# The attention prologue of a two-layer block: the kv, k_pe and query down-projections in an order written by hand

## The chip, the core and the metric

The kernel runs on one core of a Trainium2 chip. The metric is device time in microseconds (us) of one execution. TensorE (PE) does the matrix products, PEld is its weight load, VectorE (DVE) and ScalarE (ACT) do the elementwise work and read the products out of PSUM, GpSimd (POOL) does a few copies, and SyncE (SP) issues the transfers.

## The reference, cut to what matters

Two layers run over x (512 tokens of 1024 features) and a context (256 tokens). Layer 0 mixes tokens by Fourier and Hyena branches; layer 1 is latent attention, whose prologue is changed. `hx` and `hc` are the normalized and modulated rows of x and of the context.

```python
a_x = hx @ w_in                      # 256 query + 128 kv + 32 pe columns
q_x = _mla_queries(a_x[..., :256], *q_args, rope)
k_x, v_x = _mla_keys_values(a_x[..., 256:], *kv_args, rope)
a_c = hc @ w_in[:, 256:]             # the context needs kv and pe only
k_c, v_c = _mla_keys_values(a_c, *kv_args, None)
...
q   = _rms_norm(a_q, q_a_norm) @ w_uq        # latent norm over 256
ckv = _rms_norm(a_kv[..., :128], kv_a_norm)  # latent norm over 128
kv  = ckv @ w_ukv                            # keys (nope part) and values
```

Then 16 heads attend to 768 keys, the result is projected and added to x, and a gated convolutional FFN follows.

## The kernel before, in words

Features lie on partitions and tokens on the free dimension: the eight row tiles `hh[0..7]` and `hl[0..7]` (the high and the low part of h) hold 128 features each, of 512 tokens, two zero columns, 256 context tokens and two zero columns (772 in all). The context is columns 514 to 769, and its products take columns 512 to 771 (260). Every product is made of three matmuls by `mm3` (lines 121 to 125): high weight by high data (L123), high weight by low data (L124), low weight by high data (L125). A weight is loaded by `wraw`, and `wsplit` makes its two parts: ScalarE casts the high part (`hi`, L98), VectorE subtracts it for the low part (`lo`, L103). Raw, high and low weights have three buffers each.

The order of instructions on each engine is set by a scheduler that plans with its own costs, and the program's order is only one of its inputs; instructions of one engine then run strictly in the order that it wrote. PSUM has three `mm` tiles of 1024 columns and two `ms` tiles of 512.

The FFN of layer 0 ends with `norm_hook` (L283): its hook makes the first norm of layer 1 for the 512 tokens of x, and what it returns as `rest` makes the norm of the context: eight squares and sums (L233, L234), the copy of the sums, their transposes and the root (L244, L248, L250, `rsqrt` from L127), the spread of the root over the partitions (L256), and eight rows of scaled, high and low parts (L266, L267, L271).

`attention` (L959) then does, in the program's order:
- loads and splits of w_kv and w_pe (L985 on), tables for rotary embedding;
- `down(0, T)` (L1006): for each of the eight rows the kv product and the pe product, into the PSUM tiles pkv and ppe;
- `rest()`, the norm of the context;
- `latent(0, T)` (L1013): `small_norm` (L934) of kv (square L940, sum L941, copy L943, transposes L947, root L949, spread L953, copy L955), the scaling L1016, and its high and low parts kvh and kvl;
- the query products, two weights of eight rows each, into pqa;
- `down(512, 260)` and `latent(C0, C)` for the context;
- `small_norm` of the query latent, its scaling (L1044) and parts qah and qal;
- the pe part: square L1048, kp L1050, sums L1053, rotation L1058, high and low parts Kh and Kl, and POOL's copies of them (L1083);
- `values`: six token blocks by w_v (two of 512 columns each, copied out at L1028), with the load of w_uk between blocks 0 to 3 and blocks 4 and 5.

Behind it the PSUM pool is replaced, and `qk(p)` (L1091) makes queries (out `s`) and keys (out `k`) of head pair p, with two pairs made ahead of the loop over pairs.

Of the kernel before, what the change touches and what calls it, by code (L numbers as in the profile page):

```python
# [9 lines left out]
F32 = mybir.dt.float32  # L10
# [3 lines left out]
AF = mybir.ActivationFunctionType  # L14
ALU = mybir.AluOpType
# [3 lines left out]
P = 128  # L19
D = 1024  # L20
KD = 8
T = 512
C = 256
C0 = 514
# [3 lines left out]
EPS = 1e-6  # L28
# [22 lines left out]
class Builder:  # L51
# [169 lines left out]
    def norm(self, i, k, x, hh, hl, c0, n, tp):  # L221
# [31 lines left out]
        def spread(keep):  # L253
            R = self.ms()
            for b in range(n // P):
                nc.tensor.matmul(R[:, P * b : P * b + P], box["r"][:, b : b + 1].to_broadcast([P, P]), self.ident, start=True, stop=True)  # L256
            if keep:
                o = tp()
                nc.scalar.copy(o[:, :n], R[:, :n])
                R = o  # L260
            box["R"] = R

        def scaled(d):
            A, B = self.A[i][k][:, j, :], self.mod[i][:, 24 * k : 24 * k + 8, j]
            u = box[d] = tp()
            nc.vector.scalar_tensor_tensor(u[:, :n], x[d][:, c0 : c0 + n], A[:, d : d + 1], box["R"][:, :n], op0=ALU.mult, op1=ALU.mult)  # L266
            return nc.scalar.activation(hh[d][:, c0 : c0 + n], u[:, :n], AF.Identity, bias=B[:, d : d + 1])  # L267
# [15 lines left out]
    def norm_hook(self, first, second):  # L283


        s1, f1, a1 = first
        s2, f2, a2 = second

        def hook(stage, m):
            if stage == 0:  # L290
                for d in range(4) if m == 4 else (m - 1,):
                    s1(d)
            elif stage == 1:
                if m == 4:
                    s1(7)
                    f1()
                elif m == 6:
                    for d in range(4):
                        a1(d)
                elif m == 7:  # L300
                    for d in range(4, KD):
                        a1(d)

        def rest():
            for d in range(KD):
                s2(d)
            f2()
            for d in range(KD):
                a2(d)

        return hook, rest

    def zero_pads(self, tiles):
# [617 lines left out]
        self.dbg("x0", x)  # L931
        return x, hh, hl, rest

    def small_norm(self, srcs, c0, n, nfeat, tp):  # L934

        nc = self.nc
        st = self.ms()
        for i, s in enumerate(srcs):
            sq = tp()
            nc.scalar.activation(sq[:, :n], s[:, c0 : c0 + n], AF.Square)  # L940
            nc.tensor.matmul(st[0:32, :n], self.ones32, sq[:, :n], start=i == 0, stop=i == len(srcs) - 1)  # L941
        cp = tp()
        nc.scalar.copy(cp[0:32, :n], st[0:32, :n])  # L943
        nj = n // P
        rt = self.ms()
        for j in range(nj):
            nc.tensor.matmul(rt[:, j : j + 1], cp[0:32, P * j : P * j + P], self.e4[0:32, :], start=True, stop=True)  # L947
        s = self.t(self.sm, [P, 24], F32, "nrm_s")
        nc.vector.tensor_scalar(s[:, :nj], rt[:, :nj], float(D // nfeat), EPS, op0=ALU.mult, op1=ALU.add)  # L949
        r = self.rsqrt(self.sm, s, nj)  # L950
        R = self.ms()
        for j in range(nj):
            nc.tensor.matmul(R[:, P * j : P * j + P], r[:, j : j + 1].to_broadcast([P, P]), self.ident, start=True, stop=True)  # L953
        o = tp()
        nc.scalar.copy(o[:, :n], R[:, :n])  # L955
        return o


    def attention(self, x, hh, hl, rest):  # L959
        nc, I = self.nc, self.I  # L960
        v = nc.vector
        sg = ((0, 512), (512, 260))
        st = ((0, T), (C0, C))
# [8 lines left out]
        kvh, kvl = self.t(pa, [P, TW], F32R, "kvh"), self.t(pa, [P, TW], F32R, "kvl")  # L972
        qah = [self.t(pa, [P, T], F32R, f"qah{k}") for k in range(2)]
        qal = [self.t(pa, [P, T], F32R, f"qal{k}") for k in range(2)]
# [5 lines left out]
        rot, zsel, qm, ksel, s4 = msk[0:64, 0:128], msk[:, 128:130], msk[:, 256:258], msk[:, 258:260], msk[:, 260:264]  # L980
# [3 lines left out]
        tp = lambda: self.t(pt, [P, 512], F32, "pt", 4)  # L984
        wl_ = {}  # L985
        for nm_, src, n in (("kv", I["w_kv"], 1024), ("pe", I["w_pe"], 512)):
            raw = self.t(self.W, [P, 1024], F32, "wr")
            nc.sync.dma_start(raw[:, :n], src)
            h, l = self.t(pt, [P, n], F32R, "wh" + nm_, 1), self.t(pt, [P, n], F32R, "wl" + nm_, 1)
# [6 lines left out]
        for a in range(2):  # L996
            r = tp()
# [3 lines left out]
        self.zero_pads([kvh, kvl])  # L1001


        pkv, ppe = self.mm(), self.mm()

        def down(c0, n):  # L1006
            for k in range(KD):
                for ps, nm_, m in ((pkv, "kv", P), (ppe, "pe", 64)):
                    w = slice(m * k, m * k + m)
                    h, l = wl_[nm_]  # L1010
                    self.mm3(ps[:m, c0 : c0 + n], h[:, w], l[:, w], hh[k][:, c0 : c0 + n], hl[k][:, c0 : c0 + n], k == 0, k == KD - 1)

        def latent(c0, n):  # L1013
            R = self.small_norm([pkv], c0, n, P, tp)
            u = tp()
            v.scalar_tensor_tensor(u[:, :n], pkv[:, c0 : c0 + n], self.col("kvan"), R[:, :n], op0=ALU.mult, op1=ALU.mult)  # L1016
            dst = kvh[:, c0 : c0 + n]
            self.hi(dst, u[:, :n])
            self.lo(kvl[:, c0 : c0 + n], u[:, :n], dst)

        def values(js, w):
            for j in js:
                c = tok[j]
                ps = self.mm()
                for q in range(2):
                    s = slice(512 * q, 512 * q + 512)
                    self.mm3(ps[:, s], kvh[:, c : c + 128], kvl[:, c : c + 128], w[0][:, s], w[1][:, s], True, True)
                nc.scalar.copy(V[:, j, :], ps)  # L1028

        down(0, T)  # L1030
        rest()
        latent(0, T)
        pqa = self.mm()
        for m in range(2):
            wh, wl = self.wload(I["w_qa"][m])
            for k in range(KD):
                w = slice(128 * k, 128 * k + 128)
                self.mm3(pqa[:, 512 * m : 512 * m + 512], wh[:, w], wl[:, w], hh[k][:, 0:T], hl[k][:, 0:T], k == 0, k == KD - 1)
        down(512, 260)
        latent(C0, C)  # L1040
        R = self.small_norm([pqa[:, 0:512], pqa[:, 512:1024]], 0, T, 256, tp)
        for m in range(2):
            u = tp()
            v.scalar_tensor_tensor(u, pqa[:, 512 * m : 512 * m + 512], self.col("qan", m), R, op0=ALU.mult, op1=ALU.mult)  # L1044
            self.hi(qah[m], u)
            self.lo(qal[m], u, qah[m])
        sq = self.t(pt, [32, TW], F32, "sqpe", 1)
        nc.scalar.activation(sq, ppe[0:32, :TW], AF.Square)  # L1048
        kp = self.t(pt, [64, TW], F32, "kp", 1)
# [1 line left out]
        rt = self.ms()  # L1051
# [4 lines left out]
        ps = self.mm()  # L1056
        for a, m in sg:
            nc.tensor.matmul(ps[:, a : a + m], rot, kp[:, a : a + m], start=True, stop=True)  # L1058
        for a in range(2):
# [1 line left out]
            kh, kl = K[a][0]  # L1061
            self.hi(kh[rows, :], ps[rows, :TW])
            self.lo(kl[rows, :], ps[rows, :TW], kh[rows, :])
        wv = self.wload(I["w_v"])
        values(range(4), wv)
        wkh, wkl = self.wload(I["w_uk"])
        values((4, 5), wv)
        self.dbg("lat", kvh, kvl, qah, qal)
# [381 lines left out]
```

## Time and profile before

| | us |
|---|---|
| median of 3 runs | 1811.08 (1809.64 to 1812.63) |
| the profiled execution | 1817.41 |
| its span | 1815.6 |
| TensorE busy | 1707.5 (94%) |
| VectorE busy | 1019.9 (56%) |
| ScalarE busy | 614.2 (34%) |
| stretch 1024 to 1094 (prologue): TensorE, VectorE, ScalarE busy | 59.1, 39.3, 29.8 of 70 |
| granted clock in that stretch | 0.93 |
| stretch 1094 to 1386 (scores and values): TensorE busy | 267.0 of 292 |

The profiled execution is one run; all times inside it are counted from the start of its span. Views of it name an instruction by its line, its output tile, an arrow, and its inputs. Busy time is that of the instruction as the profiler models it; a wait is told with the engine whose work came last before it ended. The granted clock is the share of full speed at which TensorE's array ran.

### The profile page before, as it was taken

The page shows a single profiled execution, that of the slowest core. Times are in us where ns is not written, and L with a number is a line of the kernel's source. Part 1 is how long each engine was busy: PE and PEld are TensorE (multiplying, and loading weights), DVE is VectorE, ACT ScalarE, POOL GpSimd, SP SyncE. Part 2 cuts the span into 40 slices and gives each one's busy share as a digit, 9 for nine tenths or more (in the row PEclk, how much of TensorE's full clock was granted, in tenths as well). Part 3 has the DMA queues.
Part 4 walks back from the last instruction along what each step waited for, and adds up shares of the span by engine and source line. Part 5 has one row for each costly group of instructions (what it writes and reads, how often), then busy time and mean ns, then how long its engine had stood idle before and what let it go on. Part 6 is the DMA issues. An engine that isn't in the chain of part 4 may idle for free.

```text
span 1815.6 us, 21750 instructions
## 1 busy us (share of the span) xinstructions
PE 1707.5 (94%) x8742; PEld 1331.4 (73%) x8742; DVE 1019.9 (56%) x1662; ACT 614.2 (34%) x830; POOL 118.2 (7%) x202
## 2 busy tenths in 40 slices
PE   6889996899999999999999887899998999999999
PEld 2658875886888888888888556556555788888887
DVE  3588966936887444643333554666664554434443
ACT  3332233413322212221122334656563343223231
POOL 0042123200000000000000000100110000000000
PEclk7799997999999999999999998899999999999999
DMA  9034422332354133432312300000002322222222
GB/s 353 24 116 140 161 98 61 135 141 82 129 188 159 70 122 133 163 116 70 105 59 90 131 25 23 1 12 12 13 12 73 113 89 97 94 93 93 105 75 99
DMA packets 54977, 175.98 MB, mean 97 GB/s; under 512 B 6235, under 2 KB 9117, under 8 KB 53853
## 3 DMA queue, kind: packets, MB, share of 16 engines
q1 hardware_dynamic: 54877, 174.60, 27.7%
q8 instruction: 69, 1.13, 0.2%
q14 instruction: 31, 0.25, 0.0%
HBM read 168.81 MB, written 5.77 MB: 96 GB/s over the span
## 4 chain that ended last, share of the span: by engine, by line
PE 78%; DVE 11%; ACT 4%; issue 3%; POOL 2%; DMA 1%; POOLq 0%; SPq 0%; ACTq 0%; DVEq 0%
PE mm L123 22%; PE mm L125 21%; PE mm L124 21%; PE pv L1186 2%; DVE junk L210 2%; PE ms L234 2%; PE z L1174 2%; DVE wl L103 1%; PE s L1140 1%; DVE S L1164 1%; ACT S L1155 1%; PE s L123 1%; PE s L124 1%; PE s L125 1%; DMA wr<-wmodT 1%
## 5 line engine op out<-in xcount | busy, mean ns | idle before, releaser
L123 PE MATMUL mm<-hh,wh 128*128 128x512 f32 (+2 forms) x1344 | 476.6, 357 | 9.0 <-ACT wh L98 3.4
L124 PE MATMUL mm<-hl,wh 128*128 128x512 f32 (+2 forms) x1344 | 475.6, 355 | 5.0 <-DVE hl L271 4.8
L125 PE MATMUL mm<-hh,wl 128*128 128x512 f32 (+2 forms) x1344 | 474.8, 354 | 1.3 <-DVE wl L103 1.3
L98 ACT ACTIVATE wh<-wr 128x1024 fp32r<-128x1024 f32 (+2 forms) x200 | 206.2, 1032 | 714.3 <-PE mm L124 651.2
L103 DVE TENSOR_TENSOR wl<-wr,wh 128x1024 fp32r<-128x1024 f32 (+2 forms) x200 | 242.7, 1214 | 282.2 <-ACT wh L98 274.3
L123 PEld LDWEIGHTS mm<-hh,wh 128*128 128x128 f32 x1344 | 255.6, 191 | 60.4 <-issue 16.0
L124 PEld LDWEIGHTS mm<-hl,wh 128*128 128x128 f32 x1344 | 256.3, 191 | 43.0 <-DVE hl L271 7.7
L125 PEld LDWEIGHTS mm<-hh,wl 128*128 128x128 f32 x1344 | 255.7, 190 | 38.6 <-DVE wl L103 2.1
L123 PE MATMUL mm<-ah,wh 128*128 128x512 f32 (+1 forms) x528 | 187.8, 356 | 0.0
L124 PE MATMUL mm<-al,wh 128*128 128x512 f32 (+1 forms) x528 | 187.7, 356 | 0.0
L125 PE MATMUL mm<-ah,wl 128*128 128x512 f32 (+1 forms) x528 | 187.3, 355 | 0.0
L818 DVE SCALAR_TENSOR_TENSOR xr<-mm,mod,xr 128x512 f32<-128x512 f32 (+1 forms) x100 | 62.2, 642 | 209.2 <-PE mm L125 208.9
L210 DVE SCALAR_TENSOR_TENSOR junk<-wr,sb 128x1024 bf16<-128x1024 f32 x128 | 159.0, 1242 | 33.9 <-DMA wr<-wmodT 33.4
L123 PEld LDWEIGHTS mm<-ah,wh 128*128 128x128 f32 x528 | 99.1, 188 | 19.2 <-DVE xr L818 2.5
L124 PEld LDWEIGHTS mm<-al,wh 128*128 128x128 f32 x528 | 99.2, 188 | 15.3 <-issue 0.8
L125 PEld LDWEIGHTS mm<-ah,wl 128*128 128x128 f32 x528 | 99.2, 188 | 14.6
L1155 ACT ACTIVATE S<-s,rks 128x512 f32<-128x512 f32 x96 | 63.3, 687 | 43.4 <-PE s L125 42.5
L855 ACT ACTIVATE fg<-fg 128x772 f32<-128x772 f32 (+1 forms) x44 | 32.6, 741 | 100.0 <-DVE fg L324 89.2
L1164 DVE TENSOR_TENSOR S<-S,mb 128x1536 f32<-128x1536 f32 x32 | 54.8, 1752 | 20.7 <-POOL mb L1161 20.7
L1186 PE MATMUL pv<-S,V 128*64 128x512 f32 x192 | 59.2, 622 | 0.0
L1174 PE MATMUL z<-S,ones 128*32 128x512 f32 x192 | 43.0, 698 | 13.0 <-ACT S L1165 10.5
L1165 ACT ACTIVATE S<-S 128x1536 f32<-128x1536 f32 x32 | 47.1, 1481 | 17.7 <-DVE S L1164 17.7
(324 smaller groups left out, 2279.4 us busy)
## 6 DMA issues: line engine op xcount, KB each, us to landing
wr<-w_up SPq DMA_DIRECT2D x88, 512.0 KB, 3.2
wr<-wmodT SPq DMA_DIRECT2D x80, 512.0 KB, 3.2
wr<-w_dn SPq DMA_DIRECT2D x32, 512.0 KB, 3.2
wm<-wmod0a SPq DMA_DIRECT2D x8, 1024.0 KB, 9.5
wr<-w_in SPq DMA_DIRECT2D x16, 512.0 KB, 3.3
wr<-w_dn SPq DMA_DIRECT2D x20, 384.0 KB, 3.0
wr<-w_out SPq DMA_DIRECT2D x12, 512.0 KB, 3.3
wr<-w_o SPq DMA_DIRECT2D x12, 512.0 KB, 3.2
```

The source lines that it names most:

```text
L98: self.nc.scalar.activation(dst, src, AF.Copy)
L103: (eng or self.nc.vector).tensor_tensor(dst, src, hi.bitcast(F32), op=ALU.subtract)
L123: mmul(out, wh, xh, start=start, stop=False)
L124: mmul(out, wh, xl, start=False, stop=False)
L125: mmul(out, wl, xh, start=False, stop=stop)
L210: nc.vector.scalar_tensor_tensor(junk, raw, 1.0, self.sb[:, j, :], op0=ALU.mult, op1=ALU.mult, accum_out=acc)
L818: nc.vector.scalar_tensor_tensor(x[m][:, a2:b2], ps[:, a2:b2], mod[:, 8 * sec + m, j : j + 1], x[m][:, a2:b2], op0=ALU.mult, op1=ALU.add)
L1155: nc.scalar.activation(S[j // 3][:, j % 3, :], ps, AF.Copy, scale=rs[:, 2 * j + a : 2 * j + a + 1])
L1164: v.tensor_tensor(s, s, mb3.to_broadcast([P, 3, T]), op=ALU.subtract)
L1165: nc.scalar.activation(s, s, AF.Exp)
L1174: nc.tensor.matmul(z[32 * g : 32 * g + 32, :], self.ones32, Ss[g // 2][(2 * k + g % 2) // 3][:, (2 * k + g % 2) % 3, :], start=k == 0, sto ...
L1186: nc.tensor.matmul(pv[64 * a : 64 * a + 64, :], V[:, k, 64 * h : 64 * h + 64], Ss[a][k // 3][:, k % 3, :], start=k == 0, stop=k == 5, tile ...
```

## The change

Products for x are taken row by row of h by a helper `take`: kv and pe of row 0 and of row 1, then both query weights of rows 0 and 1, then for each further row kv, pe and the two query weights. After row 4 the sums of the context's norm stand in one block with their transposes; after row 7 come the spread and the context's rows. `rest` hands its three steps over as `rest.steps` for that. One norm is made for kv and queries together: their squares are summed on two groups of 32 partitions (`sumsq`), transposed to eight columns, and one root of eight columns is taken (`inverse_rms`); `spread` makes one tile for each. The context's kv products stand behind the sums, four rows ahead of the transposes and four behind; its pe products stand behind the sum of the context's squares. Values 0 and 1 come ahead of the spread of the context's root, 2 and 3 behind it, and the rotated pe part after them. All of this is in a block in which TensorE's order is that of the program; other engines stay with the scheduler.

```diff
@@ -308,6 +308,7 @@
             for d in range(KD):
                 a2(d)
 
+        rest.steps = second
         return hook, rest
 
     def zero_pads(self, tiles):
@@ -931,30 +932,6 @@
         self.dbg("x0", x)
         return x, hh, hl, rest
 
-    def small_norm(self, srcs, c0, n, nfeat, tp):
...
 
     def attention(self, x, hh, hl, rest):
         nc, I = self.nc, self.I
@@ -1001,22 +978,58 @@
         self.zero_pads([kvh, kvl])
 
 
-        pkv, ppe = self.mm(), self.mm()
-
-        def down(c0, n):
-            for k in range(KD):
-                for ps, nm_, m in ((pkv, "kv", P), (ppe, "pe", 64)):
-                    w = slice(m * k, m * k + m)
-                    h, l = wl_[nm_]
-                    self.mm3(ps[:m, c0 : c0 + n], h[:, w], l[:, w], hh[k][:, c0 : c0 + n], hl[k][:, c0 : c0 + n], k == 0, k == KD - 1)
-
-        def latent(c0, n):
-            R = self.small_norm([pkv], c0, n, P, tp)
+        wq_ = [self.wload(I["w_qa"][m]) for m in range(2)]
+        pkv, ppe, pqa = self.mm(), self.mm(), self.mm()
+        s2, f2, a2 = rest.steps
+
+        def take(name, k, c0, n):
+            if name == "qa":
+                for m in range(2):
+                    w = slice(128 * k, 128 * k + 128)
+                    self.mm3(pqa[:, 512 * m : 512 * m + 512], wq_[m][0][:, w], wq_[m][1][:, w], hh[k][:, c0 : c0 + n], hl[k][:, c0 : c0 + n], k == 0, k == KD - 1)
+            else:
+                ps, m = (pkv, P) if name == "kv" else (ppe, 64)
+                w = slice(m * k, m * k + m)
+                h, l = wl_[name]
+                self.mm3(ps[:m, c0 : c0 + n], h[:, w], l[:, w], hh[k][:, c0 : c0 + n], hl[k][:, c0 : c0 + n], k == 0, k == KD - 1)
+
+        def sumsq(srcs, n):
+
+            st = self.ms()
+            for g, group in enumerate(srcs):
+                for i, src in enumerate(group):
+                    sq = tp()
+                    nc.scalar.activation(sq[:, :n], src, AF.Square)
+                    nc.tensor.matmul(st[32 * g : 32 * g + 32, :n], self.ones32, sq[:, :n], start=i == 0, stop=i == len(group) - 1, tile_position=(0, 32 * g))
+            cp = tp()
+            nc.scalar.copy(cp[0 : 32 * len(srcs), :n], st[0 : 32 * len(srcs), :n])
+            return cp
+
+        def inverse_rms(cp, feats, n):
+
+            ng, nb = len(feats), n // P
+            rt = self.ms()
+            for b in range(nb):
+                nc.tensor.matmul(rt[:, ng * b : ng * b + ng], cp[0 : 32 * ng, P * b : P * b + P], s4[0 : 32 * ng, 0:ng], start=True, stop=True)
+            s = self.t(self.sm, [P, 24], F32, "nrm_s")
+            for g, nf in enumerate(feats):
+                v.tensor_scalar(s[:, g : ng * nb : ng], rt[:, g : ng * nb : ng], 1.0 / nf, EPS, op0=ALU.mult, op1=ALU.add)
+            return self.rsqrt(self.sm, s, ng * nb)
+
+        def spread(r, g, ng, n):
+            R = self.ms()
+            for b in range(n // P):
+                nc.tensor.matmul(R[:, P * b : P * b + P], r[:, ng * b + g : ng * b + g + 1].to_broadcast([P, P]), self.ident, start=True, stop=True)
+            o = tp()
+            nc.scalar.copy(o[:, :n], R[:, :n])
+            return o
+
+        def scaled(src, gain, R, dh, dl):
             u = tp()
-            v.scalar_tensor_tensor(u[:, :n], pkv[:, c0 : c0 + n], self.col("kvan"), R[:, :n], op0=ALU.mult, op1=ALU.mult)
-            dst = kvh[:, c0 : c0 + n]
-            self.hi(dst, u[:, :n])
-            self.lo(kvl[:, c0 : c0 + n], u[:, :n], dst)
+            n = src.shape[-1]
+            v.scalar_tensor_tensor(u[:, :n], src, gain, R[:, :n], op0=ALU.mult, op1=ALU.mult)
+            self.hi(dh, u[:, :n])
+            self.lo(dl, u[:, :n], dh)
 
         def values(js, w):
             for j in js:
@@ -1027,23 +1040,40 @@
                     self.mm3(ps[:, s], kvh[:, c : c + 128], kvl[:, c : c + 128], w[0][:, s], w[1][:, s], True, True)
                 nc.scalar.copy(V[:, j, :], ps)
 
-        down(0, T)
-        rest()
-        latent(0, T)
-        pqa = self.mm()
-        for m in range(2):
-            wh, wl = self.wload(I["w_qa"][m])
+        with self.tc.manual_schedule(engines={mybir.EngineType.PE}):
             for k in range(KD):
-                w = slice(128 * k, 128 * k + 128)
-                self.mm3(pqa[:, 512 * m : 512 * m + 512], wh[:, w], wl[:, w], hh[k][:, 0:T], hl[k][:, 0:T], k == 0, k == KD - 1)
-        down(512, 260)
-        latent(C0, C)
-        R = self.small_norm([pqa[:, 0:512], pqa[:, 512:1024]], 0, T, 256, tp)
-        for m in range(2):
-            u = tp()
-            v.scalar_tensor_tensor(u, pqa[:, 512 * m : 512 * m + 512], self.col("qan", m), R, op0=ALU.mult, op1=ALU.mult)
-            self.hi(qah[m], u)
-            self.lo(qal[m], u, qah[m])
+                take("kv", k, 0, T)
+                take("pe", k, 0, T)
+                if k == 1:
+                    take("qa", 0, 0, T)
+                if k:
+                    take("qa", k, 0, T)
+                if k == 4:
+                    for d in range(KD):
+                        s2(d)
+                    f2(False, 0)
+            f2(False, 1)
+            for d in range(KD):
+                a2(d)
+            cp = sumsq([[pkv[:, 0:T]], [pqa[:, 0:512], pqa[:, 512:1024]]], T)
+            for k in range(4):
+                take("kv", k, 512, 260)
+            r = inverse_rms(cp, (P, 256), T)
+            for k in range(4, KD):
+                take("kv", k, 512, 260)
+            R = [spread(r, g, 2, T) for g in range(2)]
+            for m in range(2):
+                scaled(pqa[:, 512 * m : 512 * m + 512], self.col("qan", m), R[1], qah[m], qal[m])
+            scaled(pkv[:, 0:T], self.col("kvan"), R[0], kvh[:, 0:T], kvl[:, 0:T])
+            cp = sumsq([[pkv[:, C0 : C0 + C]]], C)
+            for k in range(KD):
+                take("pe", k, 512, 260)
+            r = inverse_rms(cp, (P,), C)
+            wv = self.wload(I["w_v"])
+            values((0, 1), wv)
+            R = spread(r, 0, 1, C)
+            scaled(pkv[:, C0 : C0 + C], self.col("kvan"), R, kvh[:, C0 : C0 + C], kvl[:, C0 : C0 + C])
+            values((2, 3), wv)
         sq = self.t(pt, [32, TW], F32, "sqpe", 1)
         nc.scalar.activation(sq, ppe[0:32, :TW], AF.Square)
         kp = self.t(pt, [64, TW], F32, "kp", 1)
@@ -1061,8 +1091,6 @@
             kh, kl = K[a][0]
             self.hi(kh[rows, :], ps[rows, :TW])
             self.lo(kl[rows, :], ps[rows, :TW], kh[rows, :])
-        wv = self.wload(I["w_v"])
-        values(range(4), wv)
         wkh, wkl = self.wload(I["w_uk"])
         values((4, 5), wv)
         self.dbg("lat", kvh, kvl, qah, qal)
```

21 lines of the change are left out of this document (removed).

## The prediction

> **What bounds the kernel now.** I read the chain of work that ended last first (part 4 of the page), to see whether another engine than TensorE can set the end.
>
> ```profile
> PE 78%; DVE 11%; ACT 4%; issue 3%; POOL 2%; DMA 1%; POOLq 0%; SPq 0%; ACTq 0%; DVEq 0%
> ```
>
> TensorE sets the end, so a change counts by what it does to TensorE's waits and to its clock. The prologue that is changed is the stretch from 1024 us, where the first kv product starts, to 1094.03 us, where the first query product of head pair 0 starts (line L123, out `s`, in its timeline). From there on TensorE's order is the same in both kernels. So the question is: when does that first query product start in the new order? The windows show where the old prologue lost time (columns: window, its length, busy us of PE, PEld, DVE, ACT, POOL, then granted clock and DMA).
>
> ```profile
> 1020.00:1030.00 10.00, 5.46 (x34) 3.89 (x33) 9.05 (x15) 6.18 (x9) 2.30 (x6) 0.93 0.26 75
> 1030.00:1040.00 10.00, 8.68 (x29) 5.18 (x30) 7.21 (x10) 4.71 (x8) 0.00 (x0) 0.72 0.49 164
> ...
> 1060.00:1070.00 10.00, 8.88 (x57) 7.21 (x56) 7.06 (x17) 3.55 (x6) 0.00 (x0) 1.00 0.29 106
> 1070.00:1080.00 10.00, 6.08 (x29) 4.61 (x28) 5.30 (x14) 2.36 (x4) 3.33 (x4) 0.83 0.00 0
> 1080.00:1090.00 10.00, 9.44 (x46) 5.95 (x46) 3.11 (x15) 5.75 (x9) 0.00 (x0) 1.00 0.01 2
> ```
>
> Two dips: 1020 to 1040, where VectorE is at 9.05 of 10, and 1070 to 1080. Between them TensorE is nearly full. The waits of TensorE in the stretch 1012 to 1104 name both dips (engine line, releaser: us in total, times, longest):
>
> ```profile
> PE ms L234 <- ACT nt L233: 3.8, 1, 3.8
> PE mm L123 <- DVE rq_a L137: 3.2, 1, 3.2
> ```
>
> and TensorE's and VectorE's timelines give the prices that I use (start, us, engine, line, out<-in, count, idle before):
>
> ```profile
> 1033.04 0.80 PE L125 MATMUL mm<-hh,wlkv 128*128 128x512 f32 x1 [0.28 <-DVE wlkv L103]
> 1033.63 0.63 PE L123 MATMUL mm<-hh,whkv 128*128 128x512 f32 x1
> 1034.06 0.63 PE L124 MATMUL mm<-hl,whkv 128*128 128x512 f32 x1
> ...
> 1077.10 0.77 PE L123 MATMUL mm<-wh,kvh 128*128 128x512 f32 x1 [3.18 <-DVE rq_a L137]
> ...
> 1078.94 1.05 PE L953 MATMUL ms<-cst,rq_r 128*128 128x128 f32 x4
> ```
>
> ```profile
> 1031.77 1.21 DVE L103 TENSOR_TENSOR wlkv<-wr,whkv 128x1024 fp32r<-128x1024 f32 x1
> ...
> 1056.68 1.26 DVE L266 SCALAR_TENSOR_TENSOR nt<-xr,A,ms 128x256 f32<-128x256 f32 x3
> 1057.86 1.27 DVE L271 SCALAR_TENSOR_TENSOR hl<-nt,mod,hh 128x256 fp32r<-128x256 f32 x3
> ...
> 1059.90 1.22 DVE L103 TENSOR_TENSOR wl<-wr,wh 128x1024 fp32r<-128x1024 f32 x1
> ```
>
> The first gap ends when VectorE has split w_kv (1031.77 + 1.21 = 1032.98, TensorE resumes at 1033.04). After it, products stand 0.43 apart (1033.63, 1034.06): the clock is at half. Warm they stand 0.233 apart (1094.03, 1094.26). A 260-column product takes 0.12 warm and 0.215 at half clock (464.46 to 464.68).
>
> **The change, part by part.** The hand order holds for TensorE alone. In the built order of both kernels ScalarE and VectorE keep the scheduler's order, SP's and POOL's queues issue the same transfers and copies in the same sequence, and w_kv's split stands at the same place on VectorE. I follow TensorE's new order, each start against its releaser.
>
> 1. The first gap stays, since its end is that same split. It gets emptier: the old order put two pe products, two query products and two sums in it, and the new one, in strict row order, only two kv products. TensorE resumes at 1033.04, with 58 of the 60 products of rows 0 to 4 to do. Half clock lasted 2.9 to 5.1 us after such restarts (1077.10 to 1080.0, 463.67 to 468.8); I take 3.4, so 8 products at 0.43 = 3.4, 50 at 0.233 = 11.7, and 0.4 of waiting for the second query weight (split at 1037.36 + 1.22). Row 4 ends at 1048.6.
> 2. The context sums now stand in one block. Only three squares can be ready, as their tile `nt` has three buffers; the other five are made while TensorE waits (0.42 each, three in 1.03), then the copy of the sums (0.37) and its transposes (0.5). Three sums 0.63, five squares with their handing over 1.9, last sum 0.5, copy and transposes 0.9: 3.9, to 1052.5. Before, these sums lay between products at 0.55 each and nothing waited.
> 3. Rows 5 to 7: 36 x 0.233 = 8.4, to 1060.9. The old kernel ended the same 96 products at 1061.86, but had by then also issued the context's spread and the kv sums and transposes (0.68 + 1.04 + 1.05 us). Level so far: 1.0 ahead, 2.8 owed.
> 4. Spread 0.6. Then the joint norm's sums wait for two squares of the query latent, which on ScalarE stand behind the split of w_uk (1.06); that split waits for the last product with the first query weight, 1060.2. Squares done 1062.4, sums 1.0: 1063.5.
> 5. The context rows were made beside the second half of the query products; now no product is left to cover them. On VectorE the split of w_uk (1.22) ends at 1062.5, then 16 row operations at 0.41 (1.26 and 1.27 for three) and 0.3 for the norm's first two: 1069.5. The 24 kv context products follow row by row and end at 1069.8, instead of taking 2.9 in one piece.
> 6. The root: VectorE first splits w_uq (1.22), then 10 small operations at 0.2: 1072.8. TensorE idles from 1069.8 to 1073.0, the new 3.2 us gap, after a sparse stretch. In the old kernel such gaps dropped the clock 2.6 us in (idle from 1073.9, half from about 1076.5), and after a sparse stretch 1.3 to 1.5 us in. So I take half clock from here. Two spreads of four blocks then cost 2 x 1.95 (two blocks 1.05 in the L953 row) = 3.9, to 1076.9; warm they would be 2 x 1.0.
> 7. The context's sum is next on TensorE, and its square stands on ScalarE behind the cast of kvh: copy 0.6, two query scalings 1.5, one query split 0.7, kv scaling 0.75, cast 0.63, square 0.4 = 4.6, to 1081.5. All of it is an idle TensorE; 24 pe products that need nothing stand behind it.
> 8. Sum 0.6, 16 pe products at 0.215 = 3.4 until the clock is back (4 us, the middle of 2.9 to 5.1), 8 at 0.12 = 1.0, transposes 0.5: 1087.0.
> 9. Values 0: 1.4. Values 1 needs ppe's buffer, free when kp is made (0.2 + 0.8 + 1.0): 1089.2, ends 1090.6. Spread 0.6, values 2 and 3 2.8, sums of k_pe 1.4, rotation 1.7, values 4 and 5 2.8: 1099.9.
>
> What goes: the 3.2 us wait at 1077.10 (it was for the rotated k_pe, now made behind the values), its half clock, the separate query norm with one root (12 operations at 0.2). All that is inside the old 1094.03. What is late instead are steps 2, 5, 6 and 7. The first query product comes at 1099.9 - 1094.03 = 5.9 later, and what follows (ScalarE's copies of values 4 and 5, next weight split, square) about 0.3 more. **Sum: +6.** The profiled execution took 1817.41 (span 1815.6); it becomes 1823.4. It stood 6.3 above the median of the runs shown, 1811.08, so the median becomes 1817.
>
> [...] The rows drop the clock 1.3 to 2.6 us into a gap. [...]
>
> **The rivals.**
> A, the forecast: half clock from the gap of step 6. +6, with 4.5 to 8.5 from the unknown lengths: 2.9 to 5.1 us of slow clock (half of each difference), and 2.6 to 4.5 for step 2 (its squares hidden, or each handed over singly).
> B, the clock stays full through steps 6 to 8: the spreads cost 1.9 less and the pe products 1.6 less, so +2.5 (1.5 to 4). For it: the kv context products keep TensorE partly busy until 1069.8, and the stretch 1450 to 1454, busy to 0.4, kept clock 1.00. Against: the 3.18 us gap.
> C, the end is faster: the half clock further on goes. The query and key stage is slow from 1106.12 for 4.5 us, from 1124.15 for 3.5 and from 1144.8 for 10.2, behind waits of 3.58, 3.49 and 2.74 us. If in the new phase these waits come out below about 2.6, up to (4.5 + 3.5 + 10.2) / 2 = 9 us go; with +2.5 that is -6.5, about 1804.5. Against: these waits come from VectorE's chain within each head pair, which the change does not touch.
> D, the delay is swallowed: the wait of 3.58 at 1106.12 is for VectorE (`Kl`, L103); if VectorE comes there on its old time, TensorE gets up to 3.6 back: +2.4 or less, down to 0. Against: VectorE's chain there starts from TensorE's own query products.
> That the hand order is not what is built is ruled out by the built order.
>
> **How the numbers follow.** A 0.60, B 0.22, D 0.11, C 0.07. A measurement of this kernel can tell about 0.2% from no change, 3.6 us. Slower by more than that: nearly all of A and a third of B, 0.66; within it: the rest of B, D, a little of A, 0.27; faster: C, 0.07. The range leaves C and the lower part of D out, and goes from +1.4 (B's lower end) to +9 (A's upper end): 1812.5 to 1820.
>
> **What would show it.** Right: TensorE resumes at the w_kv split near 1033; some 3.5 us of waits on L233 and L244 near 1048 to 1052; kv context products 0.8 apart waiting for `hl` (L271); an idle 3 us ahead of line L1022 and 4 to 5 ahead of the context's L1003, with a granted clock of 0.5 around 1073 to 1085; the first query product near 1100. Wrong: full clock through 1070 to 1085 (B), a query product before 1094, or the waits at 1106 and 1124 shortened (D, C).

## The result, and the profile after

The changed kernel took 1819.58 us (median of 7 runs, 1816.27 to 1823.34), the kernel before beside it 1812.24 us (7 runs, 1804.15 to 1817.15). The ratio is 1.0047, 95% interval [1.0025, 1.0069]: slower, by 4.5 to 12.5 us. The profiled execution took 1821.08 us, its span is 1819.3 us.

The last chain's shares by engine are the same to the digit (TensorE 78%), so this is again a question of TensorE's waits and clock. First the windows (window, length, busy us of PE, PEld, DVE, ACT, POOL, granted clock, DMA share, GB/s):

```profile
1020.00:1030.00 10.00, 1.01 (x6) 0.36 (x4) 10.00 (x16) 6.72 (x11) 2.19 (x6) 0.78 0.26 73
1030.00:1040.00 10.00, 10.00 (x32) 7.11 (x33) 4.79 (x6) 2.54 (x3) 0.00 (x0) 0.71 0.65 224
...
1060.00:1070.00 10.00, 7.43 (x38) 5.02 (x34) 9.69 (x31) 4.99 (x11) 0.00 (x0) 0.83 0.21 71
1070.00:1080.00 10.00, 5.25 (x21) 4.25 (x22) 4.19 (x7) 3.69 (x7) 0.00 (x0) 0.67 0.09 34
1080.00:1090.00 10.00, 9.63 (x49) 8.30 (x48) 2.89 (x14) 3.11 (x4) 0.00 (x0) 0.82 0.01 2
```

The first dip is now a hole (1.01 us of work in ten). The second has become wide: from 1060 on VectorE works 9.69 of 10 us, and TensorE's clock is below 1 in three windows instead of one. The waits of TensorE in the stretch 1012 to 1112 name the places:

```profile
PE mm L125 <- DVE wlkv L103: 7.8, 1, 7.8
PE ms L1003 <- ACT pt L1002: 4.6, 1, 4.6
...
PE ms L1022 <- DVE rq_r L141: 1.9, 1, 1.9
```

and TensorE's timeline gives the steps (start, us, engine, line, out<-in, count, idle before and its releaser):

```profile
1029.96 0.79 PE L125 MATMUL mm<-hh,wlkv 128*128 128x512 f32 x1 [7.80 <-DVE wlkv L103]
...
1035.68 0.51 PE L123 MATMUL mm<-hh,wh 128*128 128x512 f32 x1
1036.02 0.39 PE L124 MATMUL mm<-hl,wh 128*128 128x512 f32 x1
...
1047.43 2.05 PE L234 MATMUL ms<-nt,ones 128*32 128x256 f32 x10 [0.49 <-ACT nt L233]
1049.95 0.61 PE L248 MATMUL ms<-cst,nt 128*128 128x1 f32 x4 [0.46 <-ACT nt L244]
...
1070.19 3.59 PE L1022 MATMUL ms<-cst,rq_r 128*128 128x128 f32 x16 [1.95 <-DVE rq_r L141]
1078.35 1.06 PE L1003 MATMUL ms<-pt,ones 128*32 128x256 f32 x2 [4.57 <-ACT pt L1002]
...
1097.50 0.39 PE L123 MATMUL s<-qah,wh 128*128 128x512 f32 x1
```

Products stay 0.43 apart until 1035.68, 5.7 us after the restart; the second part of the block of context sums (five sums, x10) takes 2.05 us, where five that need not wait take about 1 us, an estimate from three that take 0.56 in a kernel below; then come the root's gap and the square's.

I call **prologue** the time from the first kv product to the first query product. It is 1097.50 - 1021.43 = 76.07 us, against 1094.03 - 1024.51 = 69.52 before: **6.55 us longer**. What follows is the same: from the first query product to the span's end 721.80 us here (1819.3 - 1097.50) and 721.57 before (720.75 to 723.13 in the fourteen profiles of this study). What lies ahead is the same code too, but its end moves from execution to execution: the first kv product stands between 1015.71 and 1024.51 us in those profiles. So the length of the prologue is the clean measure of each kernel below, and a single span is not. The kernel before has one profile, so every difference in the table hangs on its 69.52.

### The profile page after: what moved, and what is told of

It is laid out like the page before. It is cut to its first block, busy times and chain, and to the rows that moved or that the text cites. A ratio compares the mean times of both kernels' runs of the same rounds, so it can differ in the third digit from the quotient of the medians.

```text
span 1819.3 us, 21726 instructions
## 1 busy us (share of the span) xinstructions
PE 1705.4 (94%) x8734; PEld 1334.2 (73%) x8734; DVE 1016.1 (56%) x1651; ACT 613.7 (34%) x829; POOL 118.1 (6%) x202
## 4 chain that ended last, share of the span: by engine, by line
PE 78%; DVE 11%; ACT 4%; issue 3%; POOL 2%; DMA 1%; POOLq 0%; SPq 0%; ACTq 0%; DVEq 0%
PE mm L123 22%; PE mm L125 21%; PE mm L124 21%; PE pv L1214 2%; DVE junk L210 2%; PE ms L234 2%; PE z L1202 2%; DVE wl L103 1%; DVE S L1192 1%; ACT S L1183 1%; PE s L1168 1%; PE s L123 1%; DVE nt L266 1%; PE s L124 1%; PE s L125 1%
## 5 line engine op out<-in xcount | busy, mean ns | idle before, releaser
L1183 ACT ACTIVATE S<-s,rks 128x512 f32<-128x512 f32 x96 | 63.4, 689 | 43.8 <-PE s L125 42.9
```

What stands on the lines that cost most here:

```text
L1183: nc.scalar.activation(S[j // 3][:, j % 3, :], ps, AF.Copy, scale=rs[:, 2 * j + a : 2 * j + a + 1])
```

## The experiments

| kernel | prologue, us | against 69.52 | ratio to the kernel before |
|---|---|---|---|
| changed kernel | 76.07 | +6.55 | 1.0047 [1.0025, 1.0069] |
| the same again | 75.90 | +6.38 | 1.0036 [1.0019, 1.0054] |
| pe products ahead of the square's sum | 73.74 | +4.22 | 1.0025 [1.0011, 1.0039] |
| pe products in the root's gap | 73.65 | +4.13 | 1.0017 [1.0004, 1.0031] |
| context sums in groups | 73.05 | +3.53 | 1.0018 [1.0006, 1.0030] |
| low parts on GpSimd, changed kernel | 73.01 | +3.49 | 1.0020 [1.0007, 1.0033] |
| no hand order, joint norm kept | 72.81 | +3.29 | 1.0019 [1.0005, 1.0032] |
| square made early, measured twice | 72.79, 72.85 | +3.3 | 1.0001 [0.9985, 1.0017], 1.0002 [0.9985, 1.0019] |
| second weight's products as cover | 72.42 | +2.90 | 1.0018 [1.0004, 1.0032] |
| hand order with its waits filled | 66.55 | -2.97 | 0.9977 [0.9962, 0.9992] |
| low parts on GpSimd, kernel before | 63.88 | -5.64 | 0.9966 [0.9954, 0.9978] |
| filled order and GpSimd | 59.39 | -10.13 | 0.9950 [0.9934, 0.9967] |

One per mille is 1.8 us. Apart from the square made early, the ratio is within 2 us of what the prologue says.

**The changed kernel again.** No edit.

> The changed kernel once more, unaltered, so that the next kernels have it beside them on the same chip. My theory (the prologue's own waits, context sums, context rows, root and context square, make it longer): the first query product comes 76 us after the first kv product, give or take 0.5, where the kernel before has 69.5, and the time stands 6 to 9 us above the kernel before (ratio 1.003 to 1.005). Rival (the difference is the phase in which the later stages meet the clock): the 76 us vary by several us between executions, or the ratio leaves 1.0025 to 1.0069.

75.90 us, with the same waits (7.84, 1.86, 4.57). In these two executions the prologue belongs to the kernel: it agrees to 0.17 us, while the first kv product stands 5.6 us earlier.

**The pe products ahead of the square's sum.**

```diff
-            cp = sumsq([[pkv[:, C0 : C0 + C]]], C)
             for k in range(KD):
                 take("pe", k, 512, 260)
+            cp = sumsq([[pkv[:, C0 : C0 + C]]], C)
```

> The 24 pe products of the context are placed ahead of the sum of the context's square, behind the two spreads. My theory (TensorE stood 4.57 us at L1003 for a square on ScalarE while 24 products that needed nothing stood behind it): the products fill this wait, the wait at L1003 falls below 1 us, and the prologue becomes about 4 us shorter than the changed kernel's 76.1: 72 us, the time 2 to 5 us above the kernel before. Rival (the wait only moves: ScalarE's chain to the cast of kvh and the values behind it set the end): the first query product stays within 1 us of 76 us and the time is that of the changed kernel. If the clock also comes back earlier because the products follow the spreads without a gap, the next stages give up to 1.5 us more.

The wait fell from 4.57 to 1.71 us, not below 1, and the prologue by 2.3 instead of 4. Counted from the first kv product, the values began 4.8 us earlier (58.64 against 63.39), and half of that was lost behind: the first values products ran slowly (0.43 apart from 1075.08 to 1078.06), and the last twelve took 4.42 us, as against 2.91 in the changed kernel, where the clock stood at 1.00; here it had halved just ahead of them. One-us windows of this kernel (columns as above):

```profile
1084.00:1085.00 1.00, 1.00 (x4) 0.37 (x2) 0.00 (x0) 0.00 (x0) 0.00 (x0) 0.99 0.00 0
1085.00:1086.00 1.00, 1.00 (x3) 0.83 (x3) 0.02 (x1) 0.81 (x1) 0.00 (x0) 0.50 0.00 0
```

TensorE counts as fully busy in both windows, and in all of 1080 to 1090 (10.00 of 10 us), and yet the clock fell to half, at 1084.98 (0.99 in that window is half clock for 0.02 us). What it does ahead of that are the k_pe sums (12 products with one column, 1.4 us) and the rotation (1.5 us). The theory of the wait holds, with a price that it did not know.

**The pe products in the root's gap.**

```diff
+            for k in range(KD):
+                take("pe", k, 512, 260)
             R = [spread(r, g, 2, T) for g in range(2)]
```

(and the same two lines away from behind the context's sum)

> The 24 pe products of the context stand between its kv products and the two spreads, that is in the 1.95 us in which TensorE waits for the root at L1022. They take 2.9 us at full clock and 5.2 at half. Theory of the forecast (the half clock of this stretch comes from the gap of the root): with the gap filled the two spreads cost 2.0 instead of 3.6 and the clock is full up to the square's wait; the prologue is 2 to 3 us shorter than the changed kernel's 76.0, 73 to 74. Rival (the clock had already fallen, at the sparse context rows before the gap): the products begin at 0.215 apart, the spreads come about as late as before, and the clock returns during the products or spreads; 74.5 to 75.5. In both the wait of some 4.6 us at L1003 stays, since nothing covers it.

73.65 us. Both were half right, as the windows show:

```profile
1068.00:1069.00 1.00, 1.00 (x7) 1.00 (x6) 0.83 (x6) 0.00 (x0) 0.00 (x0) 0.50 0.07 12
1069.00:1070.00 1.00, 1.00 (x9) 1.00 (x8) 0.69 (x5) 0.00 (x0) 0.00 (x0) 0.86 0.96 242
...
1075.00:1076.00 1.00, 0.00 (x0) 0.00 (x0) 0.96 (x2) 0.97 (x2) 0.00 (x0) 1.00 0.00 0
1076.00:1077.00 1.00, 0.00 (x0) 0.00 (x0) 1.00 (x3) 0.29 (x1) 0.00 (x0) 0.55 0.00 0
```

The clock was at half before the pe products began (1068.08), so it was not the root's gap that took it; with work in the gap it came back at 1069.3 (0.86 in that window), and the spreads took 1.95 us instead of 3.59. Then it fell again within the uncovered wait for the square (4.57), at about 1076.1 (0.55 in that window), and the first twelve values products ran slowly.

**The context sums in groups.**

```diff
-                if k == 4:
-                    for d in range(KD):
-                        s2(d)
-                    f2(False, 0)
+                for d in {1: (0, 1, 2), 3: (3, 4, 5), 4: (6, 7)}.get(k, ()):
+                    s2(d)
+                if k == 5:
+                    f2(False, 0)
```

> The eight context sums no longer stand in one block behind row 4: three stand behind row 1, three behind row 3, two behind row 4, and the transposes of the sums behind row 5. My theory (one block of sums must wait for squares, because only three of them can be ready): the waits at L234 and L248 go, the block of 4.2 us becomes about 2.2 us of sums and transposes without a wait, and the prologue becomes about 2 us shorter, 74 us. Rival (the time between row 4 and row 5 is the cost of the sums themselves, not of waiting): 76 us again. Second rival (context rows are held by VectorE, which is not reached by this): the 2 us come back as a longer wait at the context rows, L123 with hh or hl, and nothing changes at the end.

3.0 us shorter. The waits at L234 and L248 are gone (1.67 us of sums and 0.36 of transposes are left of 4.2). The second rival is there in small: the root's wait grew from 1.95 to 2.58 us. The spreads behind it took 2.54 us instead of 3.59, which gave that back and more.

**The second weight's products as cover.**

```diff
-            if name == "qa":
-                for m in range(2):
+            if name[:2] == "qa":
+                for m in [int(name[2])] if name[2:] else range(2):
...
-                    take("qa", 0, 0, T)
+                    take("qa0", 0, 0, T)
                 if k:
-                    take("qa", k, 0, T)
+                    take("qa0", k, 0, T)
...
             for d in range(KD):
                 a2(d)
+            for k in range(KD):
+                take("qa1", k, 0, T)
```

> Of the query latent's products only those with the first weight go row by row with kv and pe; the 24 with the second weight stand behind the context's spread, so that they run while VectorE makes the context rows, as in the kernel before. My theory (in the changed kernel nothing is left to cover the 6.5 us of the context rows): the context rows come out while TensorE is busy, the kv products of the context take some 3 us in one piece, the clock stays full up to them, and the prologue is 4 to 5 us shorter, 71 to 72 us. Rival (the root's chain sets the end, and it starts with the query latent's squares, which now come later): the two cancel, 75 to 77 us, and the wait at L1022 is longer by what the rows gained.

72.42 us, 3.65 shorter: the largest single gain. The context's kv products took 1.63 and 1.73 us in two pieces, the clock stood at 1.00 from 1040 to 1070, up to and through the spreads (2.02 us). It fell short by the new wait that the query squares make at the joint sum, behind a weight split and two context rows on ScalarE:

```profile
1058.89 1.90 PE L1003 MATMUL ms<-pt,ones 128*32 128x512 f32 x4 [1.21 <-ACT pt L1002]
```

**No hand order.** The same instructions and the one joint norm, ordered by the scheduler on TensorE too.

```diff
-        with self.tc.manual_schedule(engines={mybir.EngineType.PE}):
+        with ExitStack():
```

> The changed kernel with the same instructions and one joint norm, but without the hand order on TensorE: the scheduler orders it as it orders the other engines. My theory (the order costs, not the joint norm): in its built order the context sums stand among row 5's products and the context's pe products among its kv products, and a values product stands ahead of the context's sum; so the prologue is 71 to 73 us, and the time 1 to 4 us above the kernel before. Rival (one norm with one root for context and queries is what makes everything wait): 75 to 77 us as in the changed kernel.

72.81 us, as my theory had it; but it leaves 3.3 us to explain, and those are the rival's: the waits of this kernel on the chain behind the joint norm are

```profile
PE mm L123 <- ACT kvh L98: 4.3, 1, 4.3
...
PE ms L1022 <- DVE rq_r L141: 3.0, 1, 3.0
```

7.3 us, where the longest wait of the kernel before behind a root is 3.2. So about half of the 6.5 us goes with the hand order. That the other half is the one late norm, which puts the kv scaling, and with it the values, behind the query products, is argued from these waits and not shown: 1.5 of the 3.3 us are slow last values products as above, and no run has the new order with two norms.

**The low parts of the two down weights on GpSimd**, in the changed kernel and in the kernel before.

```diff
-            self.lo(l, raw[:, :n], h)
+            self.lo(l, raw[:, :n], h, nc.gpsimd)
```

> The changed kernel, with the low parts of the two down weights (w_kv, w_pe) made on GpSimd instead of VectorE, where they stood behind row operations. My theory (the first gap of 7.8 us ends at that split on VectorE, a GpSimd operation on 128x512 took 1.3 to 1.6 us here, so that w_kv's 128x1024 should take about 3): TensorE resumes some 4 to 5 us earlier, then meets the low part of the first query weight, which VectorE makes after its rows: 2 to 3 us shorter, 73 to 74 us. Rival (GpSimd and VectorE hold each other up: VectorE's row operations get longer while GpSimd runs): the resume is earlier but the rows of h come later, under 1 us gained.

> The kernel before, with the low parts of the two down weights (w_kv, w_pe) made on GpSimd instead of VectorE. My theory: its TensorE order has all kv and pe products ahead of the query products, so that the first gap (5.7 us of waits between 1024.5 and 1033.0) goes but for the pace of h's rows; the prologue falls from 69.5 to 64 to 66 us and the time by 4 to 6 us, ratio 0.9967 to 0.998. Rival (VectorE is the limit there, by the rows of h that it makes, 9 of 10 us busy): the products then wait row by row and 1 to 2 us are gained at most, ratio above 0.999.

73.01 and 63.88 us. In the kernel before it is worth 5.6 us; in the changed one 3.1, since its strict row order then stands 2.57 us for the low part of the query weight. The GpSimd row and a VectorE row beside it, both of the kernel before so edited:

```profile
1016.00 2.42 POOL L103 TENSOR_TENSOR wlkv<-wr,whkv 128x1024 fp32r<-128x1024 f32 x1 [1.16 <-ACT whkv L98]
```

```profile
1016.78 2.20 DVE L271 SCALAR_TENSOR_TENSOR hl<-nt,mod,hh 128x512 fp32r<-128x512 f32 x1
```

GpSimd takes 2.42 us for what VectorE did in 1.21, and one VectorE row beside it took 2.20 us instead of 0.75, as the next but one took 1.68 beside w_pe's split on GpSimd (1.27); but it starts with the first kv product (1016.00 and 1015.98), where VectorE came to this split 7.3 us behind it (1031.77 and 1024.51).

**The context's square made early**, measured twice.

```diff
+            cc = sumsq([[pkv[:, C0 : C0 + C]]], C)
             R = [spread(r, g, 2, T) for g in range(2)]
...
-            cp = sumsq([[pkv[:, C0 : C0 + C]]], C)
...
-            r = inverse_rms(cp, (P,), C)
+            r = inverse_rms(cc, (P,), C)
```

> The sum of the context's square is placed right behind the context's kv products, ahead of the two spreads, in the text and in TensorE's order. ScalarE stood idle from 1066.5 to 1072.4 in the changed kernel, so the square (0.36 us) can be made there and its sum lies in the root's gap. My theory (the 4.57 us wait at L1003 was only the place of the square behind the casts on ScalarE): the wait goes, the pe products follow the spreads, and the values then wait for kvl at most 1 us: the prologue is 70.5 to 73, the time 1 to 3 us above the kernel before. Rival (the square cannot be made earlier, because the work tiles or the sums' banks are taken until the spreads are copied): the wait turns up ahead of the spreads and 75 to 77 us stay.

> The kernel with the context's square ahead of the spreads once more, since its time (ratio 1.0001) and its prologue (72.8 us, 3.3 more than the kernel before) agreed badly. Theory (the prologue decides, and the executions of that call happened to lie low): the prologue is 72.3 to 73.3 us again and the ratio 1.001 to 1.0025. Rival (the prologue differs between executions, by the half clock in which the last 12 values products of this trace stood 0.43 apart): the prologue of this trace is some 1.5 to 3 us shorter and the ratio stays below 1.001.

The wait of 4.57 us at L1003 became 0.53, so it was only the place of the square on ScalarE. What is late next is kvh, which ScalarE casts behind the query latent's casts and another square:

```profile
PE mm L123 <- ACT kvh L98: 1.6, 1, 1.6
...
PE ms L1003 <- ACT pt L1002: 0.5, 1, 0.5
```

The prologue is 72.8 us in both traces, 1.5 of it in slow last values products as above. The time is another matter: 1.0001 and 1.0002, that is 0.2 to 0.4 us over the kernel before where the prologue says 3.3; the upper bounds, 1.0017 and 1.0019, come to 3.1 and 3.4 us, one just below it and one just above. So the theory of the second measurement held for the prologue and missed on the ratio (1.001 to 1.0025 expected). The two profiled executions took 1815.59 and 1819.23 us and are among the slowest of the twelve beside them (medians 1808.91 and 1810.86). Whether the other executions kept their clock in this stretch can't be seen; this stays open.

**The filled order, without and with GpSimd.** Both put the grouped sums, the cover and the early square together, and scale kv ahead of the queries; the one with GpSimd also has kv and pe of all rows ahead of the query products. The core is

```diff
+            for k in range(KD):
+                take("qa1", k, 0, T)
+            for k in range(4):
+                take("kv", k, 512, 260)
             cp = sumsq([[pkv[:, 0:T]], [pqa[:, 0:512], pqa[:, 512:1024]]], T)
-            for k in range(4):
-                take("kv", k, 512, 260)
-            r = inverse_rms(cp, (P, 256), T)
             for k in range(4, KD):
                 take("kv", k, 512, 260)
+            r = inverse_rms(cp, (P, 256), T)
+            for k in range(KD):
+                take("pe", k, 512, 260)
+            cc = sumsq([[pkv[:, C0 : C0 + C]]], C)
             R = [spread(r, g, 2, T) for g in range(2)]
+            scaled(pkv[:, 0:T], self.col("kvan"), R[0], kvh[:, 0:T], kvl[:, 0:T])
             for m in range(2):
                 scaled(pqa[:, 512 * m : 512 * m + 512], self.col("qan", m), R[1], qah[m], qal[m])
-            scaled(pkv[:, 0:T], self.col("kvan"), R[0], kvh[:, 0:T], kvl[:, 0:T])
-            cp = sumsq([[pkv[:, C0 : C0 + C]]], C)
-            for k in range(KD):
-                take("pe", k, 512, 260)
-            r = inverse_rms(cp, (P,), C)
+            r = inverse_rms(cc, (P,), C)
```

> The hand order with its waits filled, all in one: context sums in groups among rows 1, 3 and 4; the second query weight's 24 products behind the context's spread; the joint sums among the context's kv products; the 24 pe products and the context's square and sum in the root's gap; the kv latent scaled ahead of the query latent. My theory (the joint norm in a hand order lost only through the waits that stood open in it; single edits gave 2.3 to 3.6 us each): the prologue is 60 to 65 us, shorter than the 69.5 of the kernel before, and the time 4 to 9 us below it, ratio 0.995 to 0.998. Rival (one chain from the last query product through squares, sums, root, spread, scaling and cast, about 11 us, sets the values whatever is put into it): 67 to 70 us, ratio 0.9985 to 1.0005.

> As the filled hand order, and the low parts of the two down weights made on GpSimd; kv and pe products of all rows stand ahead of the query products, the context sums among rows 4 to 7. My theory (the two gains are in different places and add: the split gave the kernel before 5.6 us): the prologue is 54 to 60 us and the time 10 to 15 us below the kernel before, ratio 0.992 to 0.9945. Rival (with kv and pe alone, TensorE only keeps pace with the rows of h that VectorE makes, and the context sums wait for squares): 60 to 64 us, no better than the GpSimd split in the kernel before.

66.55 us without GpSimd: between the theory (60 to 65) and its rival (67 to 70), with 1.5 us of slow last values products in it. The ratio 0.9977 [0.9962, 0.9992] lies in the theory's range. So a hand order with the joint norm can beat the kernel before. With GpSimd 59.39 us and 1801.51 us (median of 6 runs, 1800.20 to 1802.01), the kernel before beside it 1810.70: ratio 0.9950 [0.9934, 0.9967], the fastest version of this study. The prologue is the theory's; the gain, 9.2 us, falls just short of the 10 to 15 expected. In its waits (1012 to 1093) nothing of the chain behind the norm is over 1 us:

```profile
PE mm L125 <- POOL wlkv L103: 1.8, 1, 1.8
...
PE ms L1022 <- DVE rq_r L141: 1.0, 1, 1.0
PE ms L1003 <- ACT pt L1002: 0.8, 1, 0.8
PE mm L123 <- ACT kvh L98: 0.8, 1, 0.8
```

## Which steps of the prediction held, and which failed

The direction was right, and so were the first gap, the block of sums and the wait for the square, with their releasers. What failed is the length of the half clock in steps 1 and 8, the cause of it in step 6, and what holds up TensorE at the end of step 5. By its steps, each end counted from the first kv product (the prediction's time less 1024.51, the trace's less 1021.43):

| step | predicted end | measured end | what differed |
|---|---|---|---|
| 1 first gap, rows 0 to 4 | 24.1 | 24.8 | half clock for 5.7 us, not 3.4 |
| 2 context sums | 28.0 | 29.0 | 4.2 us, not 3.9 |
| 3 rows 5 to 7 | 36.4 | 37.4 | 8.46 us, not 8.4 |
| 4 spread, joint sums | 39.0 | 40.1 | 2.7 us, not 2.6 |
| 5 context rows | 45.3 | 46.8 | 6.7 us, not 6.3; clock halved at its end |
| 6 root, spreads | 52.4 | 52.4 | gap 1.95, not 3.2; spreads 3.59, not 3.9 |
| 7 wait for the square | 57.0 | 56.9 | 4.57 us, not 4.6 |
| 8 sum, pe, transposes | 62.5 | 63.4 | half clock for 5.2 us after the restart, not 4 |
| 9 values to the first query product | 75.4 | 76.1 | 12.7 us, not 12.9 |

**Steps 2, 5, 7 are shown.** Taking each away alone shortened the prologue by 3.0, 3.65 and 2.3 to 3.3 us. Of the 3.5 us of waits expected in step 2 the view names 0.95 (0.49 and 0.46); about 1 more, an estimate, lies inside the second part of the block. The square of step 7 stands where it was expected, behind the casts on ScalarE:

```profile
1075.34 1.29 ACT L98 ACTIVATE qah<-pt 128x512 fp32r<-128x512 f32 x2 [0.89 <-DVE pt L1030]
1077.39 0.63 ACT L98 ACTIVATE kvh<-pt 128x512 fp32r<-128x512 f32 x1 [0.76 <-DVE pt L1030]
1077.93 0.36 ACT L1002 ACTIVATE pt<-mm 128x256 f32<-128x256 f32 x1
```

**What failed is the size of the half clock, in steps 1 and 8.** I took 3.4 and 4 us of it behind a restart, bounded by 2.9 and 5.1 us from the trace of before; the trace shows 5.7 and 5.2, both beyond the upper bound. In step 1 this cost 1.0 us more than I had, of which 0.4 came back because the wait for the second query weight did not occur; step 8 took 1.0 us more. That is some 1.7 us of the level, given back in part by step 6, so that the prologue grew by 6.55 instead of 5.9.

A length counted from the restart was the wrong quantity. These windows of the changed kernel (columns as above) hold its changes of clock between 1066 and 1084; in all windows between them the clock is 0.50 or 1.00:

```profile
1066.00:1067.00 1.00, 1.00 (x8) 1.00 (x9) 1.00 (x5) 0.52 (x2) 0.00 (x0) 0.81 0.00 0
...
1073.00:1074.00 1.00, 0.78 (x5) 0.59 (x4) 0.00 (x0) 0.13 (x1) 0.00 (x0) 0.78 0.00 0
...
1076.00:1077.00 1.00, 0.00 (x0) 0.00 (x0) 1.00 (x2) 0.63 (x1) 0.00 (x0) 0.93 0.00 0
...
1083.00:1084.00 1.00, 1.00 (x8) 1.00 (x7) 0.00 (x0) 0.00 (x0) 0.00 (x0) 0.66 0.00 0
```

A granted 0.81 is half clock for 0.38 us of the window, so the clock fell at 1066.62, and in the same way it rose at 1073.44, fell at 1076.86 and rose at 1083.68: 6.82, 3.42 and 6.82 us apart. Worked out like this from windows of half a us, the changes between 1000 and 1130 us (eight in the kernel before, nine in the changed one) lie on a grid with steps of 3.41 us, to 0.01 us, in each of the two profiles. So each half clock in these stretches lasted one to three steps from its fall (three of them, 10.24 us, from 1025.66 to 1035.90 around the first gap), and what was left of it behind a restart followed from where in a step the restart came: 2.8 us at the 1077.10 of the kernel before, where the clock rose at 1079.89, and 5.3 at the 1078.35 here, where it rose at 1083.68.

**Step 6 came out at the right time by the wrong cause.** Its gap was 1.95 us, and the half clock was there before it, at the end of the context rows:

```profile
1066.57 0.37 PE L125 MATMUL mm<-hh,wlkv 128*128 128x260 f32 x1
1066.74 0.42 PE L123 MATMUL mm<-hh,whkv 128*128 128x260 f32 x1
```

The pe products in the root's gap showed it in another way: the clock was at half when they began. In the changed kernel it fell at these rows, at 1066.62, and stayed at half through the gap, until 1073.44. It could also have come out otherwise: with the context sums in groups the same rows, with the same waits of 0.43 and 0.25 us, ran at full clock (0.12 apart from 1061.89 to 1062.85), and it fell at about 1067.2 (0.86 granted from 1060 to 1070), in the spreads behind the gap. The gap was short because TensorE came late to it, not because the root came early: the spreads began 48.8 us after the first kv product, against 48.5 predicted.

**Step 5 ended on TensorE, not on VectorE.** Its sign, kv context products 0.8 us apart that wait for `hl`, did not come: the trace has two waits there, 0.43 for `hh` and 0.25 for `hl`. The joint norm's transposes, 1.05 us between these products (L1013), were left out of this step, and the last products ran at half clock, so that the last one ended at 1068.24, 1.2 us behind VectorE's last row (1067.04).

**The level.** The median came out 2.6 us above the 1817.0 predicted. 1.2 us of this is the kernel before, whose median was 1812.24 beside the changed one and 1811.08 in the three runs that I had; 0.8 is the prologue and what follows (6.55 + 0.23 against 6.0); the remaining 0.6 is less than the interval of the ratio can tell. The median lies only 0.4 us below the range's top, 1820.0, and three of the seven executions, the profiled one among them (1821.08), lie above it. The range held the unknown lengths of the slow clock, but not that executions of one kernel lie 13 us apart (1804.15 to 1817.15); in the profiles 8.8 us of such a spread lie ahead of the first kv product.

**The rivals.** B (full clock through 1070 to 1085) did not occur: the windows have 0.67 and 0.82, with full clock from 1073.44 to 1076.86 and again only from 1083.68. C and D did not: the query and key stage keeps its waits (3.57 and 3.48 us behind VectorE's `Kl`, 2.74 next), and the time behind the prologue is the same to 0.23 us. The clock fell at 1066.62, with no idle time of TensorE longer than 0.43 us in the five us before, and at 1076.86, about 3.1 us into the gap that began at 1073.78.

## What to carry to other kernels

An order written out for one engine has to be checked against the order that the others keep: for each block, ask which of its inputs can be ready when it starts, and put products that need nothing into every such wait rather than behind it. Here a hand order with the joint norm cost 6.5 us with its waits open and gained 3.0 with them filled. And measure the stretch that changes, between two instructions that both kernels have: in the two kernels profiled twice it repeated to 0.2 us, where whole executions differed by 13.

## What the runs showed of the hardware that was not expected

- In the profiles of the kernel before and of the changed one the clock changed only on a grid with steps of 3.41 us (seventeen changes between 1000 and 1130 us). After the 7.80 us gap the slow products went on for 5.7 us without a wait (1029.96 to 1035.68); in the kernel before, whose gap held a few products, for 4.6 us from the sums at 1031.03 (to 1035.66).
- Half clock came without a gap. In five traces (pe products first, no hand order, square early both times, filled order) the twelve k_pe sums and the rotation, in which TensorE is recorded as busy throughout, were followed by slow products (0.43 apart) for some 3 us; in the other seven traces with this tail, the changed kernel's among them, the products behind the same instructions stood 0.233 apart. The cost is 1.5 us. With the pe products first the clock fell at 1084.98, 2.86 us into these instructions (from 1082.12); in the changed kernel it stood at 1.00 through the same ones (from 1091.68) and the products behind them. What separates the two groups is not shown: no run moved these instructions alone.
- A VectorE operation of 0.75 us took 2.20 us beside a GpSimd operation of 2.42 us, yet moving the work to GpSimd gained 5.6 us, because it was the starting time that counted: level with the first kv product instead of 7.3 us behind it.
